# Bias table in bfloat16 column parts, one rwkv gate for four pairs, and a regrouped inversion copy in a two-block network

## The chip, the cores and the metric

The kernel runs on one core of one Trainium2 chip. The metric is the device time of one execution in microseconds (us), lower is better; of several executions the median counts. The engines are TensorE (PE in the profile, with PEld for its weight loads), VectorE (DVE), ScalarE (ACT), GpSimd (POOL) and SyncE (SP, which here only starts DMA transfers).

## The reference, cut to what matters

The network takes 256 tokens of width 1024 through a first block (swiglu feed-forward, a mixer, a second feed-forward) and then two layers of a second block. Three places of it are touched. The first is the rwkv mixer of the first block, above all its gate `g` and its scan:

```python
p = token_shift(p.astype(jnp.float32), mu)
r, k, v, wd, ad, gd = _split_last(
    p, (RWKV_WIDTH, RWKV_WIDTH, RWKV_WIDTH, DECAY_LORA, AAA_LORA, GATE_LORA))
...
g = jax.nn.sigmoid(gd) @ g2          # gd: 256 tokens x 160, g2: 160 x 1024
...
wkv = wkv7_scan(rh, heads(decay), kh, vh, -kk, kk * ah)
...
return (y + bonus.reshape(B, S, RWKV_WIDTH)) * g
```

The second is the bias of the second block's attention, a table of 32 buckets by 8 heads, looked up by the distance of two positions:

```python
def _t5_bias(table, q_pos, k_pos):
    bucket = _t5_bucket(q_pos[:, :, None] - k_pos[:, None, :])
    return jnp.transpose(table[bucket].astype(jnp.float32), (0, 3, 1, 2))
```

## The kernel before

A float32 product is computed on TensorE as three products of float32r operands: each operand is split into a high part (a cast on ACT, L241) and the rest (a subtraction on DVE, L242), and `mm3` (L293 to L295) issues high by high, low by high and high by low. Weights stream through `wload`: SP loads a piece of up to 128x1024 into the ring `wraw` of four buffers, and the split writes the rings `whi` and `wlo`, four buffers each. In the first feed-forward a second ring of raw buffers lets SP run further ahead. The PSUM tiles come from rings too: `acc` (3), `pin` (3), `po` (1) and `pt` (1).

Every engine executes its own instructions strictly in their order. That order isn't the order of the source: a scheduling pass decides it when the program is built, so a change of one place moves instructions around it. Outside of the first feed-forward and the mixer the two programs have the same order.

**Bias table.** While the first feed-forward runs, `bias_steps` (L1138) builds a bias table `bt` in DRAM, in six blocks, about one in each of the feed-forward's eleven column steps. A block is 2048 columns: POOL subtracts the positions (`d`, L1163), DVE compares with the thresholds (`ind`, L1166: 1 where the distance reaches a bucket), and TensorE multiplies `ind` by differences of the table, so that the sum over the reached buckets is the bucket's value. The table's differences are split in two float32r terms, so a block takes four groups of two matmuls (L1170, L1171) of 512 columns. All write the 32 partitions 0 to 31 of a `pt` tile, and after each group ACT copies them (L1172). Four DMAs issued by POOL (L1175) then store the block.

**Mixer.** `mix1` runs eight rwkv pairs (two heads each) in up to three lanes at once, beside a side lane with the dilated attention and the gates, from which TensorE gets dense matmuls to do. `rwkv_setup` computes the inputs of the small matrices once: `lora` matmuls for two halves of the tokens (t), ACT copies the result to `lt` (L727), PE transposes it (L735 to L737), and shift, tanh and a scale make `wdad`, `sga` (128 rows of gd) and `sgb` (32 rows). The gate is computed in each pair: `rwkv_norm` multiplies `sga` and `sgb` by the pair's 128 columns of g2 in plain float32 (L781, L782; a float32 matmul shows as two records), for both halves t, into an `acc` tile that is held until the last multiplication of the pair (L789). The weights g2a and g2b come on ACT's DMA queue.

**Inversion.** Each pair inverts triangular 64x64 matrices in levels (L903 to L937). A level above the first computes eight small products (L908) and two transposes of G (L913) into two `acc` tiles, ACT copies both to `PT`, and the next products (L931) need all of `PT`. The products of o=0 (upper rows) and the transposes share the tile q[0], six blocks wide (copied at L917); those of o=1 have q[1], two blocks wide (copied at L918).

Of the kernel before, what the change touches and what calls it, by code (L numbers as in the profile page):

```python
# [108 lines left out]
def layout(i):  # L109
# [25 lines left out]
    pc[:32, P_MUL + 2] = mu[3328:3360]  # L135
# [9 lines left out]
    o['m_g2'] = i['rwkv_g2'][0]  # L145
# [46 lines left out]
class Net:  # L192
# [518 lines left out]
    def rwkv_setup(self, xT):  # L711
# [13 lines left out]
        lt = rp.tile([128, 2, 512], F32, name="lt", tag="AL", bufs=2)[:, :, :288]  # L725
        for t in range(2):
            nc.scalar.copy(lt[:, t], pins[t])  # L727
        self.wdad = rp.tile([128, T], F32, name="wdad")
        self.sga = rp.tile([128, T], F32, name="sga")
        self.sgb = rp.tile([32, T], F32, name="sgb")  # L730
        p = self.acc([2, T])
        p2 = self.acc([T])
        for t in range(2):
            s = slice(t * 128, t * 128 + 128)
            nc.tensor.transpose(p[:, 0, s], lt[:, t, 0:128], self.idn)  # L735
            nc.tensor.transpose(p[:, 1, s], lt[:, t, 128:256], self.idn)
            nc.tensor.transpose(p2[0:32, s], lt[:, t, 256:288], self.idn)  # L737
        self.shift(self.wdad, p[:, 0], pc[:, P_MUL:P_MUL + 1], om[:, 24:25])
        self.shift(self.sga, p[:, 1], pc[:, P_MUL + 1:P_MUL + 2], om[:, 25:26])
        self.shift(self.sgb, p2[0:32], pc[0:32, P_MUL + 2:P_MUL + 3], om[0:32, 26:27])  # L740
        nc.scalar.activation(self.wdad[0:64], self.wdad[0:64], AF.Tanh)
        for sg in (self.sga, self.sgb):
            nc.scalar.activation(sg, sg, AF.Tanh, scale=0.5)
            nc.vector.tensor_scalar(sg, sg, 0.5, 0.5, op0=ALU.mult, op1=ALU.add)

# [7 lines left out]
    def rwkv_gate(self, hf):  # L753
        nc, rp = self.nc, self.rp
        cs = slice(hf * 512, hf * 512 + 512)
        g2a = rp.tile([128, 512], F32, name="g2a")
        g2b = rp.tile([32, 512], F32, name="g2b")
        nc.scalar.dma_start(g2a, self.I['m_g2'][0:128, cs])
        nc.scalar.dma_start(g2b, self.I['m_g2'][128:160, cs])
        return g2a, g2b, self.gb('m_lnw', 512, 512 * hf), self.gb('m_lnb', 512, 512 * hf)  # L760

    def rwkv_norm(self, yt, vt, bs, pl, g2a, g2b, lnw, lnb):
# [6 lines left out]
        sq = rp.tile([128, 2, 128], F32, name="gsq")  # L769
# [19 lines left out]
        nc.vector.tensor_mul(yt, yt, g)  # L789

    def rwkv_pair(self, p, pl, xT, yt, w2a2, gate):
# [106 lines left out]
        for lv in range(1, 6):  # L898
# [4 lines left out]
            q = [self.acc([4, 64])] if lv == 1 else [self.acc([6, 64]), self.acc([2, 64])]  # L903
# [945 lines left out]
```

## Time and profile before

| what | value |
|---|---|
| median of three executions | 2522.95 us (2520.93 to 2526.31) |
| profiled execution | 2529.44 us |
| its span (first to last instruction) | 2527.7 us |
| mean granted TensorE clock | 0.988 of 2.4 GHz |
| PE busy | 2445.9 us (97%) |
| DVE, ACT, POOL busy | 1123.1, 894.9, 127.1 us |

Busy time counts each instruction from its start to its end. TensorE overlaps matmuls, so two neighbours' starts tell more of what a matmul costs than its own duration. The granted clock is told for stretches: 1.0 is 2.4 GHz, 0.5 is 1.2 GHz. Times in the rows are counted from the first instruction.

### The profile page before, as it was taken

Reading aid. Unit: us, or ns where it says so; the run is one execution under the profiler, and the core shown is the slowest. Engines: PE = TensorE matmul, PEld = TensorE weight load, DVE = VectorE, ACT = ScalarE, POOL = GpSimd, SP = SyncE. Lnnn points to the kernel's source line nnn. Section 1 sums busy time; section 2 is a strip of 40 time slices with the busy share of each in tenths; the row PEclk is TensorE's granted clock in tenths of the full one; section 3 lists DMA queues with packets and bytes.
Section 4 is the critical chain, followed back from the end, with each engine's and each line's share of the span. In section 5 each row is a group of like instructions: output and inputs, shape, how many; then the busy total and the mean of one; then the engine's idle time right before and its main releaser. Section 6 shows DMA issues by size and latency. Waiting matters only on the chain. (4 is left out here: it accounts for less than half of the span.)

```text
span 2527.7 us, 49959 instructions
## 1 busy us (share of the span) xinstructions
PE 2445.9 (97%) x20537; PEld 1739.7 (69%) x20537; DVE 1123.1 (44%) x1991; ACT 894.9 (35%) x1652; POOL 127.1 (5%) x167
## 2 busy tenths in 40 slices
PE   8999999999999999999999999899999999999997
PEld 6778888877788898788888977654356346535631
DVE  7655777665655566875557486401110110000002
ACT  5445544444444466644445564200100010000000
POOL 3200101000000000000001000200000000000000
PEclk9999999999999999999999999999999999999998
DMA  7554222126555454466545435799999999999997
GB/s 271 181 182 154 79 74 84 44 88 233 168 194 191 128 193 134 149 233 200 188 131 185 147 120 178 274 380 394 409 407 399 361 408 393 380 383 408 407 395 293
DMA packets 174379, 607.79 MB, mean 240 GB/s; under 512 B 20288, under 2 KB 25152, under 8 KB 173760
## 3 DMA queue, kind: packets, MB, share of 16 engines
q1 hardware_dynamic: 163872, 584.06, 63.6%
q10 hardware_dynamic: 9232, 18.69, 2.3%
q8 instruction: 163, 2.67, 0.4%
q0 software_dynamic: 1040, 1.78, 0.3%
q14 instruction: 72, 0.59, 0.1%
HBM read 600.78 MB, written 3.67 MB: 239 GB/s over the span
## 5 line engine op out<-in xcount | busy, mean ns | idle before, releaser
L242 DVE TENSOR_TENSOR wlo<-wraw,whi 128x1024 fp32r<-128x1024 f32 (+3 forms) x462 | 554.7, 1205 | 371.0 <-ACT whi L241 360.7
L241 ACT CAST whi<-wraw 128x1024 fp32r<-128x1024 f32 (+3 forms) x462 | 464.5, 1008 | 457.4 <-PE pin L295 225.8
L564 PE MATMUL pin<-wraw,xg 128*32 128x256 f32 (+1 forms) x6272 | 557.0, 411 | 2.3 <-DMA wraw<-e_in 2.3
L564 PEld LDWEIGHTS pin<-wraw,xg 128*32 128x32 f32 (+1 forms) x6272 | 253.0, 113 | 241.1 <-issue 113.5
L293 PE MATMUL pin<-whi,xh 128*128 128x512 f32 (+3 forms) x1088 | 410.3, 377 | 3.2 <-ACT plt L1461 1.4
L294 PE MATMUL pin<-wlo,xh 128*128 128x512 f32 (+3 forms) x1088 | 407.8, 375 | 5.0 <-DVE wlo L242 5.0
L295 PE MATMUL pin<-whi,xl 128*128 128x512 f32 (+3 forms) x1088 | 406.8, 374 | 2.2 <-DVE xl L242 2.1
L549 PE MATMUL acc<-wraw,hT 128*32 128x256 f32 (+1 forms) x3136 | 282.6, 411 | 3.2 <-ACT hT L539 1.7
L572 DVE TENSOR_TENSOR h<-pin,sg 128x256 f32<-128x256 f32 (+1 forms) x84 | 29.9, 378 | 573.8 <-ACT sg L571 573.8
L293 PEld LDWEIGHTS pin<-whi,xh 128*128 128x128 f32 x1088 | 206.4, 190 | 42.1 <-issue 5.6
L295 PEld LDWEIGHTS pin<-whi,xl 128*128 128x128 f32 x1088 | 206.1, 189 | 41.7 <-issue 6.5
L294 PEld LDWEIGHTS pin<-wlo,xh 128*128 128x128 f32 x1088 | 206.4, 190 | 40.0 <-DVE wlo L242 8.7
L549 PEld LDWEIGHTS acc<-wraw,hT 128*32 128x32 f32 (+1 forms) x3136 | 124.8, 113 | 109.3 <-issue 39.8
L571 ACT ACTIVATE sg<-pin 128x256 f32<-128x256 f32 (+1 forms) x84 | 29.4, 350 | 430.7 <-PE pin L564 429.0
L293 PE MATMUL pin<-xh,whi 128*128 128x256 f32 x448 | 131.9, 294 | 0.0
L294 PE MATMUL pin<-xl,whi 128*128 128x256 f32 x448 | 130.2, 291 | 0.0
L295 PE MATMUL pin<-xh,wlo 128*128 128x256 f32 x448 | 128.8, 287 | 0.0
L539 ACT COPY hT<-pt 128x384 f32<-128x384 f32 (+1 forms) x56 | 23.9, 427 | 236.7 <-PE pt L537 236.7
L294 PEld LDWEIGHTS pin<-xl,whi 128*128 128x128 f32 x448 | 86.3, 193 | 1.6 <-issue 0.3
L295 PEld LDWEIGHTS pin<-xh,wlo 128*128 128x128 f32 x448 | 86.4, 193 | 0.7
L293 PEld LDWEIGHTS pin<-xh,whi 128*128 128x128 f32 x448 | 86.3, 193 | 0.7
L295 PE MATMUL acc<-whi,hl 128*128 128x512 f32 x198 | 77.5, 392 | 1.0 <-DVE hl L242 0.9
(524 smaller groups left out, 3097.9 us busy)
## 6 DMA issues: line engine op xcount, KB each, us to landing
wraw<-e_in SPq DMA_DIRECT2D x448, 512.0 KB, 8.7
wraw<-e_out SPq DMA_DIRECT2D x224, 512.0 KB, 8.7
wraw<-ffn_in SPq DMA_DIRECT2D x88, 512.0 KB, 4.1
wraw<-ffn_out SPq DMA_DIRECT2D x44, 512.0 KB, 3.6
wraw<-d_in SPq DMA_DIRECT2D x44, 512.0 KB, 4.3
wraw<-l_dqk SPq DMA_DIRECT2D x32, 512.0 KB, 3.9
wraw<-l_gate SPq DMA_DIRECT2D x32, 512.0 KB, 3.7
wraw<-m_rkv SPq DMA_DIRECT2D x24, 512.0 KB, 3.7
```

Source lines behind the costliest of these rows:

```text
L241: nc.scalar.copy(hi, src)
L242: nc.vector.tensor_sub(lo, src, hi.bitcast(F32))
L293: mm(out, lh, rh, start=start, stop=False, skip_group_check=True)
L294: mm(out, lh, rl, start=False, stop=False, skip_group_check=True)
L295: mm(out, ll, rh, start=False, stop=stop, skip_group_check=True)
L539: nc.scalar.copy(hT[d], pt)
L549: mm(acc[r // per][P[c], r % per], t[:, r * nt + i, P[u]], w[:, n * c:n * c + n], start=d + g + k == 0 and r % per == 0, stop=d == NG // 2 ...
L564: mm(pin[r // per][P[c], r % per].rearrange("p (a c) -> p a c", a=2), xg[:, kc, W * r:W * r + W], v[c * 2 // C][:, c % (C // 2)], start=kc ...
L571: nc.scalar.activation(sg, q[:, :, 0:nh], AF.Silu)
L572: nc.vector.tensor_mul(hs[d][:, b[0]:b[-1] + 1], q[:, :, nh:n], sg)
```

## The change

The bias table's differences become three bfloat16 terms, `ind` becomes bfloat16, and each of a block's four column groups writes 32 partitions of its own: twelve matmuls of 512 columns, term by term over the four column parts, into one `pt` tile, one copy of 128x512, and sixteen stores instead of four. The gate is computed once for four pairs (for 512 columns of g2) with float32r splits, in `rwkv_gate`: its weights come through `wload`, five matmuls of 512 columns for each half t write a `pin` tile, and ACT copies it to SBUF. The rows of `sgb` are duplicated to 64, so that one matmul takes the high and low part. In the inversion the transposes go into the same tile as the products of o=1, whose copy now comes second.

```diff
@@ layout
-    pc[:32, P_MUL + 2] = mu[3328:3360]
+    pc[:64, P_MUL + 2] = np.tile(mu[3328:3360], 2)
...
-    o['m_g2'] = i['rwkv_g2'][0]
+    g2 = np.zeros((2, 128, 1024), np.float32)
+    for hf in range(2):
+        w = i['rwkv_g2'][0][:, 512 * hf:512 * hf + 512]
+        g2[hf, :, :512] = w[:128]
+        g2[hf, :64, 512:] = np.tile(w[128:160], (2, 1))
+    o['m_g2'] = g2
@@ rwkv_setup
-            nc.scalar.copy(lt[:, t], pins[t])
+            nc.scalar.copy(lt[:, t, 0:288], pins[t])
+            nc.scalar.copy(lt[:, t, 288:320], pins[t][:, 256:288])
...
-            nc.tensor.transpose(p2[0:32, s], lt[:, t, 256:288], self.idn)
+            nc.tensor.transpose(p2[0:64, s], lt[:, t, 256:320], self.idn)
...
+        self.sga = [rp.tile([128, T], F32R, name="sga" + e) for e in "hl"]
+        self.split(*self.sga, sga)
+        self.sgb = rp.tile([64, T], F32R, name="sgb")
+        nc.scalar.copy(self.sgb, sgb)
+        nc.vector.tensor_sub(self.sgb[32:64], sgb[32:64], self.sgb[32:64].bitcast(F32))
@@ rwkv_gate
-        g2a = rp.tile([128, 512], F32, name="g2a")
-        g2b = rp.tile([32, 512], F32, name="g2b")
-        nc.scalar.dma_start(g2a, self.I['m_g2'][0:128, cs])
-        nc.scalar.dma_start(g2b, self.I['m_g2'][128:160, cs])
-        return g2a, g2b, self.gb('m_lnw', 512, 512 * hf), self.gb('m_lnb', 512, 512 * hf)
+        (wh, wl), = self.wload(self.I['m_g2'][hf], 1024, [1024])
+        gate = rp.tile([128, 2, 512], F32, name="gate")
+        f = dict(start=False, skip_group_check=True)
+        for t in range(2):
+            s = slice(t * 128, t * 128 + 128)
+            g = self.pin([512])
+            self.mm3(g, self.sga[0][:, s], self.sga[1][:, s], wh[:, 0:512], wl[:, 0:512], True, False)
+            nc.tensor.matmul(g, self.sgb[:, s], wh[0:64, 512:1024], stop=False, **f)
+            nc.tensor.matmul(g, self.sgb[0:32, s], wl[0:32, 512:1024], stop=True, **f)
+            nc.scalar.copy(gate[:, t], g)
+        return gate, self.gb('m_lnw', 512, 512 * hf), self.gb('m_lnb', 512, 512 * hf)
@@ rwkv_norm
-        g = self.acc([2, 128])
-        cs = slice(128 * pl, 128 * pl + 128)
-        for t in range(2):
-            s = slice(t * 128, t * 128 + 128)
-            nc.tensor.matmul(g[:, t], self.sga[:, s], g2a[:, cs], start=True, stop=False)
-            nc.tensor.matmul(g[:, t], self.sgb[:, s], g2b[:, cs], start=False, stop=True)
...
-        nc.vector.tensor_mul(yt, yt, g)
+        nc.vector.tensor_mul(yt, yt, gate[:, :, 128 * pl:128 * pl + 128])
@@ rwkv_pair, a level of the inversion
-            q = [self.acc([4, 64])] if lv == 1 else [self.acc([6, 64]), self.acc([2, 64])]
+            q = [self.acc([4, 64])] if lv == 1 else [self.acc([2, 64]), self.acc([6, 64])]
...
-                    nc.tensor.transpose(q[0][:, 2 + 2 * j:4 + 2 * j].rearrange("p a b -> p (a b)"),
+                    nc.tensor.transpose(q[1][:, 2 + 2 * j:4 + 2 * j].rearrange("p a b -> p (a b)"),
...
-                    nc.scalar.copy(PT[R, 0:6, 0:n], q[0][R, :, 0:n])
-                    nc.scalar.copy(PT[R, 6:8, 0:n], q[1][R, :, 0:n])
+                    nc.scalar.copy(PT[R, 6:8, 0:n], q[0][R, :, 0:n])
+                    nc.scalar.copy(PT[R, 0:6, 0:n], q[1][R, :, 0:n])
@@ bias_steps
-            tbh, tbl = pp.tile([128, 32], F32R, name="tbh"), pp.tile([128, 32], F32R, name="tbl")
+            tb3 = pp.tile([128, 3, 32], BF16, name="tb3")
...
-                    ind = pp.tile([128, 2048], F32R, name="ind")
-                    out = pp.tile([32, 2048], F32, name="bo")
+                    ind = pp.tile([128, 2048], BF16, name="ind")
+                    out = pp.tile([128, 512], F32, name="bo", bufs=2)
...
+                    q = self.pt([512])
+                    for m in range(3):
+                        for n in range(4):
+                            nc.tensor.matmul(q[32 * n:32 * n + 32], tb3[:, m], ind[:, n * 512:n * 512 + 512],
+                                             start=m == 0, stop=m == 2, skip_group_check=True)
+                    nc.scalar.copy(out, q)
+                    m = ni // 4
                     for n in range(4):
-                        s = slice(n * 512, n * 512 + 512)
-                        q = self.pt([512])
-                        nc.tensor.matmul(q[0:32], tbh, ind[:, s], start=True, stop=False)
-                        nc.tensor.matmul(q[0:32], tbl, ind[:, s], start=False, stop=True)
-                        nc.scalar.copy(out[:, s], q[0:32])
-                    for g in range(4):
-                        r = 128 * t + 32 * g + i0
-                        nc.gpsimd.dma_start(self.bt[:, r:r + ni, :nk], out[8 * g:8 * g + 8].rearrange("p (i k) -> p i k", k=nk))
+                        for g in range(4):
+                            nc.gpsimd.dma_start(bt[t, g, :, i0 + n * m:i0 + n * m + m, :nk],
+                                                out[32 * n + 8 * g:32 * n + 8 * g + 8].rearrange("p (i k) -> p i k", k=nk))
```

The scheduler's order moves at the mixer's start. On PE before, the transposes of the first half of `lt` were followed by the first matmuls of pair 0's r projection (`pin<-xh,whi`, weights m_rkv), then came the transposes of the second half:

```order
L295 MATMUL pin<-whi,xl 128x288
L735 MATMUL acc<-c,lt 128x128
L736 MATMUL acc<-c,lt 128x128
L737 MATMUL acc<-c,lt 32x128
L293 MATMUL pin<-xh,whi 128x256
L294 MATMUL pin<-xl,whi 128x256
L295 MATMUL pin<-xh,wlo 128x256
...
L735 MATMUL acc<-c,lt 128x128
```

Now, at the same place on PE, with the lines of the changed kernel (L298 to L300 are `mm3`, L741 to L743 the transposes, L826 and L827 the decay matmuls of pair 0, L775 and L776 the gate's matmuls with `sgb`):

```order
L743 MATMUL acc<-c,lt 64x128
L826 MATMUL acc<-wdad,w2a_2082 128x256
L827 MATMUL acc<-wdad,w2a_2082 128x256
L298 MATMUL pin<-whi,sgah 128x512
L299 MATMUL pin<-wlo,sgah 128x512
L300 MATMUL pin<-whi,sgal 128x512
L298 MATMUL pin<-whi,sgah 128x512
L775 MATMUL pin<-whi,sgb 128x512
L776 MATMUL pin<-wlo,sgb 128x512
...
L298 MATMUL pin<-xh,whi 128x256
```

Both halves' transposes, the decay matmuls and all ten gate matmuls of the first four pairs now stand ahead of pair 0's projections; the decay matmuls stood behind them before.

ACT feeds these matmuls. Before, from the copy of the second half of `lt` on, it had this order (`sga` and `sgb` are done with their tanh, L743):

```order
L727 COPY lt<-pin 128x288
L241 CAST whi<-wraw 128x768
L597 ACTIVATE wdad<-acc,om 128x256
L597 ACTIVATE sgb<-acc,om 32x256
L597 ACTIVATE sga<-acc,om 128x256
L741 ACTIVATE wdad<-wdad 64x256
L743 ACTIVATE sgb<-sgb 32x256
L597 ACTIVATE rT<-pin,om 128x256
L241 CAST whi<-wraw 128x768
L743 ACTIVATE sga<-sga 128x256
```

Now ACT has, from the casts of the gate's weights and of the first two m_rkv pieces (x3) on:

```order
L246 CAST whi<-wraw 128x1024 x3
L732 COPY lt<-pin 128x288
L733 COPY lt<-pin 128x32
L246 CAST whi<-wraw 128x1024
L602 ACTIVATE wdad<-acc,om 128x256
L602 ACTIVATE sg_2055<-acc,om 64x256
L602 ACTIVATE sg_2055<-acc,om 128x256
L747 ACTIVATE wdad<-wdad 64x256
...
L829 ACTIVATE tw<-acc,hw 128x256
L755 CAST sgb<-sg_2055 64x256
L246 CAST sgah<-sg_2055 128x256
```

Pair 0's tanh (`tw`, L829) and the two casts that the gate needs have come in behind the chain; two more tanhs stand where the dots are.

In the inversion, ACT's copies of one level stood in either order before, here with the wide one first:

```order
L917 COPY PT<-acc 128x384
L918 COPY PT<-acc 128x128
L241 CAST whi<-wraw 128x1024
L597 ACTIVATE kT<-pin,om 128x256
L945 COPY XYr<-acc 128x2x64
```

The same place now:

```order
L929 COPY PT<-acc 128x128
L930 COPY PT<-acc 128x384
L829 ACTIVATE tw<-acc,hw 128x256
L832 ACTIVATE sq<-kT,pc 128x256
L830 ACTIVATE ta<-acc,hw 128x256
```

Of the 24 levels of full height (three in each pair) 14 had the narrow copy last; now none has.

## Rows read from the trace of the kernel before

**Rows 1.** The page's busy times, shares of the span and instruction counts.

```profile
PE 2445.9 (97%) x20537; PEld 1739.7 (69%) x20537; DVE 1123.1 (44%) x1991; ACT 894.9 (35%) x1652; POOL 127.1 (5%) x167
```

**Rows 2.** Stretch, its us; busy PE, PEld, DVE, ACT, POOL; granted clock, DMA share, GB/s.

```profile
11.00:216.00 205.00, 200.61 (x887) 158.10 (x887) 129.42 (x134) 104.47 (x143) 40.39 (x39) 0.99 0.56 184
216.00:560.00 344.00, 333.52 (x4140) 281.94 (x4139) 235.19 (x597) 171.32 (x417) 39.33 (x54) 0.97 0.29 91
```

**Rows 3.** Timeline of PE in a bias block: start us, duration us, engine, line, what.

```profile
45.39 0.40 PE L1170 MATMUL pt<-ind,tbh 128*32 128x512 f32 x1
45.62 0.39 PE L1171 MATMUL pt<-ind,tbl 128*32 128x512 f32 x1
45.85 0.39 PE L293 MATMUL pin<-whi,xh 128*128 128x512 f32 x1
```

**Rows 4.** Weight loads of line L1170: count, duration ns min/median/max, first and last start.

```profile
L1170 PEld LDWEIGHTS pt<-ind,tbh x24: 106/106/108, 45.2 to 151.9; 128*32 128x32 f32 x24
```

**Rows 5.** Timeline of PE in the experts, where four column parts take turns.

```profile
1699.50 3.21 PE L564 MATMUL pin<-wraw,xg 128*32 128x256 f32 x56
```

**Rows 6.** Timeline of POOL in the bias blocks, idle time before in brackets.

```profile
51.59 2.46 POOL L1175 DMA_DIRECT2D bt<-bo  x4 [14.95 <-ACT bo L1172]
54.07 3.62 POOL L1163 TENSOR_TENSOR d<-pq,pr 128x2048 int32<-128x2048 int32 x1
71.66 2.40 POOL L1175 DMA_DIRECT2D bt<-bo  x4 [13.98 <-ACT bo L1172]
```

**Rows 7.** Timeline of DVE at the same place.

```profile
51.95 1.22 DVE L242 TENSOR_TENSOR wlo<-wraw,whi 128x1024 fp32r<-128x1024 f32 x1
54.06 4.72 DVE L242 TENSOR_TENSOR wlo<-wraw,whi 128x1024 fp32r<-128x1024 f32 x1 [0.89 <-ACT whi L241]
```

**Rows 8.** Timeline of PE, the gate of the first pair and what follows it.

```profile
314.14 0.38 PE L781 MATMUL acc<-g2a,sga 128*128 128x128 f32 x2
...
315.70 0.46 PE L908 MATMUL acc<-G,AL 64*64 64x64 f32 x16
```

**Rows 9.** Timeline of PE, the gate of the fifth pair.

```profile
459.14 0.74 PE L781 MATMUL acc<-g2a,sga 128*128 128x128 f32 x2
```

**Rows 10.** Busy time and granted clock (PEclk) of three short stretches, columns as in rows 2.

```profile
216.00:220.00 4.00, 2.54 (x14) 1.66 (x13) 4.00 (x7) 2.92 (x7) 0.00 (x0) 0.99 0.68 216
220.00:223.00 3.00, 3.00 (x11) 2.90 (x11) 2.12 (x7) 0.42 (x1) 0.74 (x2) 0.50 0.99 345
...
459.00:469.00 10.00, 10.00 (x64) 8.30 (x64) 6.16 (x20) 2.13 (x5) 2.79 (x4) 0.50 0.01 2
```

**Rows 11.** Timeline of PE at the mixer's start.

```profile
237.01 0.37 PE L293 MATMUL pin<-xh,whi 128*128 128x256 f32 x1
...
238.15 0.28 PE L295 MATMUL pin<-xh,wlo 128*128 128x256 f32 x1
239.46 0.33 PE L735 MATMUL acc<-c,lt 128*128 128x128 f32 x1 [1.04 <-ACT lt L727]
...
239.77 0.36 PE L293 MATMUL pin<-xh,whi 128*128 128x256 f32 x1
```

**Rows 12.** Timeline of ACT at the mixer's start.

```profile
238.06 1.05 ACT L241 CAST whi<-wraw 128x1024 fp32r<-128x1024 f32 x1 [1.08 <-DMA wraw<-m_rkv]
239.02 0.39 ACT L727 COPY lt<-pin 128x288 f32<-128x288 f32 x1
...
240.04 0.48 ACT L597 ACTIVATE wdad<-acc,om 128x256 f32<-128x256 f32 x1
...
243.15 0.41 ACT L743 ACTIVATE sga<-sga 128x256 f32<-128x256 f32 x1
```

**Rows 13.** Timeline of ACT, the two copies of one level of the inversion.

```profile
303.68 0.50 ACT L917 COPY PT<-acc 128x384 f32<-128x384 f32 x1
304.15 0.27 ACT L918 COPY PT<-acc 128x128 f32<-128x128 f32 x1
```

**Rows 14.** Waits of the weight loads from 220 to 560: total us, times, longest.

```profile
PEld acc L931 <- ACT PT L917: 1.5, 6, 0.3
```

More of the change, by code (lines that the diff above doesn't have):

```diff
@@ L724, in rwkv_setup @@
         self.gemm(pins, xT, 8, [I['m_lora'][0, c] for c in range(2)], 288, 4, tiles=True)
-        lt = rp.tile([128, 2, 512], F32, name="lt", tag="AL", bufs=2)[:, :, :288]
+        lt = rp.tile([128, 2, 512], F32, name="lt", tag="AL", bufs=2)[:, :, :320]
         for t in range(2):
-            nc.scalar.copy(lt[:, t], pins[t])
+            nc.scalar.copy(lt[:, t, 0:288], pins[t])
+            nc.scalar.copy(lt[:, t, 288:320], pins[t][:, 256:288])
         self.wdad = rp.tile([128, T], F32, name="wdad")
-        self.sga = rp.tile([128, T], F32, name="sga")
-        self.sgb = rp.tile([32, T], F32, name="sgb")
+        sg2 = rp.tile([128, 2, T], F32, name="sg2", tag="AL", bufs=2)
+        sga, sgb = sg2[:, 0], sg2[0:64, 1]
         p = self.acc([2, T])
@@ L736, in rwkv_setup @@
             nc.tensor.transpose(p[:, 1, s], lt[:, t, 128:256], self.idn)
-            nc.tensor.transpose(p2[0:32, s], lt[:, t, 256:288], self.idn)
+            nc.tensor.transpose(p2[0:64, s], lt[:, t, 256:320], self.idn)
         self.shift(self.wdad, p[:, 0], pc[:, P_MUL:P_MUL + 1], om[:, 24:25])
-        self.shift(self.sga, p[:, 1], pc[:, P_MUL + 1:P_MUL + 2], om[:, 25:26])
-        self.shift(self.sgb, p2[0:32], pc[0:32, P_MUL + 2:P_MUL + 3], om[0:32, 26:27])
+        self.shift(sga, p[:, 1], pc[:, P_MUL + 1:P_MUL + 2], om[:, 25:26])
+        self.shift(sgb, p2[0:64], pc[0:64, P_MUL + 2:P_MUL + 3], om[0:64, 26:27])
         nc.scalar.activation(self.wdad[0:64], self.wdad[0:64], AF.Tanh)
-        for sg in (self.sga, self.sgb):
+        for sg in (sga, sgb):
             nc.scalar.activation(sg, sg, AF.Tanh, scale=0.5)
             nc.vector.tensor_scalar(sg, sg, 0.5, 0.5, op0=ALU.mult, op1=ALU.add)
+        self.sga = [rp.tile([128, T], F32R, name="sga" + e) for e in "hl"]
[3 more added lines that the diff above has]
+        nc.vector.tensor_sub(self.sgb[32:64], sgb[32:64], self.sgb[32:64].bitcast(F32))
     def rwkv_open(self, hf):
@@ L755, in rwkv_gate, with rwkv_norm @@
         cs = slice(hf * 512, hf * 512 + 512)
-        g2a = rp.tile([128, 512], F32, name="g2a")
-        g2b = rp.tile([32, 512], F32, name="g2b")
-        nc.scalar.dma_start(g2a, self.I['m_g2'][0:128, cs])
-        nc.scalar.dma_start(g2b, self.I['m_g2'][128:160, cs])
-        return g2a, g2b, self.gb('m_lnw', 512, 512 * hf), self.gb('m_lnb', 512, 512 * hf)
-    def rwkv_norm(self, yt, vt, bs, pl, g2a, g2b, lnw, lnb):
+        (wh, wl), = self.wload(self.I['m_g2'][hf], 1024, [1024])
[9 more added lines that the diff above has]
+        return gate, self.gb('m_lnw', 512, 512 * hf), self.gb('m_lnb', 512, 512 * hf)
+    def rwkv_norm(self, yt, vt, bs, pl, gate, lnw, lnb):
         nc, rp = self.nc, self.rp
@@ L768, in rwkv_norm @@
         mean, var = rp.tile([128, 2, 2], F32, name="gmean"), rp.tile([128, 2, 2], F32, name="gvar")
-        sq = rp.tile([128, 2, 128], F32, name="gsq")
+        sq = rp.tile([128, 2, 128], F32, name="gsq", tag="sq", bufs=1)
         nc.vector.tensor_reduce(mean, v4(yt), AX, ALU.add)
@@ L930, in rwkv_pair @@
                         for o in range(2):
-                            mm(d[r][B(o), j], PT[B(r), 2 + 2 * j + o, 0:n], PT[B(r), 6 * o + j, 0:n], start=True, stop=True)
+                            mm(d[r][B(o), j], PT[B(r), 2 + 2 * j + o, 0:n], PT[B(r), 6 - 6 * o + j, 0:n], start=True, stop=True)
                 for r in range(2):
@@ L1154, in bias_steps @@
             nc.vector.tensor_sub(tb[:, 0], tb[:, 0], tb[:, 1])
-            self.split(tbh, tbl, tb[:, 0])
+            for n in range(3):
+                nc.vector.tensor_copy(tb3[:, n], tb[:, 0])
+                if n < 2:
+                    nc.vector.tensor_sub(tb[:, 0], tb[:, 0], tb3[:, n])
+            bt = self.bt.rearrange("h (t g i) k -> t g h i k", t=2, g=4)
             for t in range(2):
```

## The prediction

> **What bounds the kernel now.** I read the page's busy times first. TensorE is busy for 97% of the span, DVE for 44%, ACT for 35% [rows 1]. The windows by stretch then say whether that holds where the change works. In the first feed-forward PE is busy for 200.6 of 205 us, with DVE at 129 and ACT at 104; among the rwkv pairs it is 333.5 of 344, with DVE at 235 and ACT at 171 [rows 2]. So both stages wait for PE, and the question for each edit is how much PE time it frees or how long it makes PE stand. Busy counts a matmul until its modelled end, so I price matmuls by the distance of two starts on the timeline, not by their durations.
>
> **The bias table.** A matmul of 512 columns lasts 0.39 us, but the next starts 0.23 us after it [rows 3]. There are 24 of each of the two lines, as the weight loads of one show [rows 4], so before the six blocks cost 48 x 0.23 = 11.0 us of PE. Now they have 72 matmuls. All write 32 partitions, four neighbours four different column parts. The nearest thing in the trace is the expert stage, which has float32 matmuls in four column parts: 56 records of 256 float32 columns lie in 3.21 us [rows 5]. Less about 0.4 for the last one's own duration that leaves 2.8 us for 13 steps of four records, 0.218 us a step. One float32r matmul of 512 columns takes 0.23, so a step of four costs what a single matmul of 512 columns does: the four column parts run side by side there. By that row 72 matmuls are 18 groups of 0.218, 3.9 us; the edit frees 7.1 us. That they don't run side by side is a rival below. I take the experts' row since it has the same column parts and a step of the same length.
>
> What else a block does lies under PE's work. ACT has one copy of 512 columns in place of four. DVE's comparison writes bfloat16 in place of float32r; its cost isn't shown, from nothing to twice a like instruction, and DVE is idle for 76 of 205 us [rows 2]. POOL issues sixteen DMAs in place of four: 2.46 us become 4 x 2.46 = 9.8, and the subtraction behind them, 3.62 us, starts later [rows 6]. Together they are 13.4 us, and blocks come every 20.1 us (51.59 to 71.66), so POOL keeps pace and the store of the table, needed only by the second block, can't be late. One thing could hurt: while POOL subtracts, a DVE subtraction takes 4.72 us in place of 1.22 [rows 7], 3.5 us longer. The pause is there before as well, only at another place relative to PE. I count nothing for moving it; a rival has its price.
>
> **The gate.** Before, a pair's eight records take 314.14 to 315.70, 1.56 us at full clock [rows 8]. Seven pairs make 10.9 us. The fifth runs in a stretch granted 0.50, that is 1.2 GHz, and its first two records take 0.74 in place of 0.38 [rows 9, 10]; I count it double, 3.1, so 14.0 us in all. Now there are twenty matmuls of 512 columns, 20 x 0.23 = 4.6 us. PE is freed of 9.4 us. The weights' splits (two casts, two subtractions) and four copies are ACT and DVE work of about 1 us each, under PE's, as [rows 2] show these engines' idle time; without that cover the second gate would cost PE one cast and two copies, some 2 us.
>
> **The wait at the mixer's start.** This speaks against the change. The order shows that ten gate matmuls and the decay matmuls now stand ahead of pair 0's projections on PE, and whatever is behind them waits as well. Before, PE began these projections at 237.01, worked until 238.15, waited until 239.46 for the copy of the second half of `lt`, and went on at 239.77 [rows 11]. That copy itself was late by a weight cast whose DMA had not landed: the cast starts at 238.06, the copy at 239.02 [rows 12]. Now, in the times of before: the copy starts at 239.02; with the small one behind it (0.2, an estimate from half the big one's 0.39) ACT is free at 239.6. The order puts one more weight cast there, 1.05, so the chain starts at 240.65. Before, the first and the eighth ACT instruction of this place started at 240.04 and 243.15 [rows 12]; one of the seven steps is a weight cast of 768 columns (0.8, an estimate from 1.05 for 1024), which leaves 2.3 for six, 0.39 each. Nine of them (three shifts, three tanhs, `tw`, two casts) take 3.5, to 244.2, and the subtractions of the low parts on DVE take two such steps more, to 245.0. Then seven of the ten gate matmuls are left, 1.6, and the projections start at 246.6: 9.6 us later than before. Of this, 2.3 is the gate (counted above), about 1.0 are ten transpose and decay records that before stood elsewhere (three transposes take 0.31, 239.46 to 239.77), and 1.2 is the old wait, gone. PE stands 5.1 us longer. Bounds: 4.0, if the missing DMA lands earlier (ACT waited 1.08 for it [rows 12], and ACT's queue no longer loads gate tables); 6.1, if one more cast of 1.05 gets in.
>
> **The clock.** After 216 to 220, in which PE was busy for only 2.54 of 4 us, the granted clock fell to 0.50 [rows 10]. The new wait leaves PE emptier than that. The fall costs nothing while PE waits and half of what it does afterwards; for the 3 us after that wait which the rows show at 0.50, 1.5 us. Bounds: nothing, and half of a stretch of 10 us like that at 459, 5.0 [rows 10].
>
> **The inversion.** The narrow copy behind the wide one made `PT` ready at 304.42 in place of 304.18 [rows 13]. In 14 of 24 levels it stood so; that is 0.24 x 14 = 3.4 us over the chains of all pairs, in up to three lanes under PE's other work. What PE's weight loads waited for the wide copy is 1.5 us [rows 14]. Bounds: nothing and 1.5; I take 0.8, the middle, for nothing tells which of the six waits had the narrow copy in the way. Which lane gets an `acc` tile when also changes, and I have no row for a price of that.
>
> **Sum**, against the profiled execution's 2529.44: -7.1 - 9.4 + 5.1 + 1.5 - 0.8 = -10.7, to 2518.7. The median of before is 6.5 below that execution; the same difference from 2522.95 gives **2512.2 us**, 0.4% less. About 0.2% (5 us) is what a measurement of this kernel can tell from no change.
>
> **Rivals.** *One after another* (slower). If each weight load of a bias matmul waits until the matmul before it has ended, nothing overlaps: 12 x (0.39 + 0.11) = 6.0 us a block by [rows 3, 4], 36.0 in place of 11.0. The sum becomes 7.1 + 25.0 - 10.7 = +21.4, 2544.4. The other four terms make -3.6, so the kernel gets slower from 1.83 + 3.6 / 6 = 2.4 us a block on, and by more than 0.2% from 3.3. Against it: [rows 5], where loads belong to column parts too. If only the array is shared in turn, at 0.23 each, the blocks cost 72 x 0.23 = 16.6 and the sum is 5.6 - 3.6 = +2.0, 2525.0. The Trainium skill, page "TensorE: Matmul & The Clock Gate", Part 3 on packing small matmuls, has a rule for this rival: a weight load overlaps matmuls in flight only when its row group differs, and here all of them use the same rows; by that rule the time would be this rival's 2544, and [rows 5], where neighbours use the same rows too, do not bear it out. The same part also tells of 2.38 times the speed with three column parts, by which the twelve matmuls would overlap.
>
> *DVE's pause* gets in PE's way: of the six subtractions the four that stand behind a block's stores move, and each keeps a weight's low part back for the 3.5 us of [rows 7], +14.0, 2526.3. For it: PE has few pieces in stock. Against it: the same pause came before and PE's share of that stage is 98% [rows 2].
>
> *A deeper start*: wait 6.1, clock 5.0, the second gate uncovered 2.0, no gain in the inversion: -3.4 in sum, 2519.6.
>
> *A lighter start*: wait 4.0, no fall of the clock, inversion 1.5: -14.0, 2509.0; and if the slow stretch of 459 to 469 leaves together with the old gate's records in it, 5.0 less, 2504.
>
> *It does not do what it says*: the copies' order is free already. That is 0.8 of my sum and changes no verdict.
>
> **Chances.** My forecast 0.58, the lighter start 0.10, the deeper one 0.16, DVE's pause 0.06, turns in the array 0.04, one after another 0.06. The range from 2504 to 2522 takes in the two starts and leaves out the last three rivals, 0.16, and little below. Within 0.2% (2517.9 to 2528.0) end the deeper start, the pause, the turns and 0.03 of my forecast: 0.29. Faster: 0.65. Slower: 0.06.
>
> **What would show it.** In the changed profile, a block's twelve matmuls start within about 0.7 us (2.8 or 6 for the first rival); the lines L781 and L782 are gone and ten matmuls with `sgah`, `sgal` and `sgb` of about 0.23 us each stand in two places; PE has a hole of some 6 us around 230 to 240, before pair 0's projections, and the clock is 0.50 after it; POOL's DMAs take about 10 us a block; the stages after the mixer last as before. I am wrong if PE's hole is filled by other work or grows to twice that, or if the rwkv pairs with their new order wait more on each other than these rows let me see.

## The result, and the profile after

The changed kernel takes **2552.03 us** (median of 5 runs, 2547.50 to 2554.34); the kernel before, on the same chip, 2524.67 (2520.93 to 2526.31). The ratio is 1.0106 (95% interval 1.0094 to 1.0117): some 27 us slower, where 11 us faster was forecast. In the text, shares of a ratio are turned into time with 2524 us. The profiled execution of the changed kernel took 2552.97 us, its span is 2551.0.

First the page's busy times and the two stretches of [rows 1, 2], in the changed kernel:

```profile
PE 2453.5 (96%) x20517; PEld 1745.1 (68%) x20517; DVE 1127.6 (44%) x1999; ACT 888.9 (35%) x1643; POOL 163.5 (6%) x239
```

```profile
11.00:216.00 205.00, 199.70 (x944) 158.88 (x943) 136.08 (x154) 98.97 (x132) 77.24 (x113) 1.00 0.60 195
216.00:560.00 344.00, 323.80 (x3960) 271.57 (x3959) 221.45 (x553) 166.13 (x400) 37.55 (x50) 0.93 0.27 82
```

The first stretch is as full as before. In the second, PE is busy 10 us less and at a lower granted clock, 0.93 in place of 0.97. Most of the loss is there.

The bias table answers to [rows 3, 4]. PE's timeline in one block, and the rows of its line in the whole program (count, duration ns min/median/max, first and last start):

```profile
44.91 0.83 PE L1187 MATMUL pt<-ind,tb 128*32 128x512 bf16 x12
45.67 0.51 PE L298 MATMUL pin<-whi,xh 128*128 128x512 f32 x1
```

```profile
L1187 PEld LDWEIGHTS <-tb x72: 92/95/97, 44.9 to 134.5; 128*32 128x32 bf16 x72
L1187 PE MATMUL pt<-ind,tb x72: 379/379/389, 44.9 to 134.8; 128*32 128x512 bf16 x72
```

Twelve matmuls that last 0.38 each hold PE for 0.76 us (44.91 to 45.67): the column parts run side by side, and six blocks cost 4.6 us in place of 11.0.

The mixer's start answers to [rows 11]. PE's timeline: the first half's transposes, the second half's, the decay matmuls, the first gate matmul, pair 0's first projection. Under it two stretches of windows (columns as in [rows 2]):

```profile
228.50 0.27 PE L741 MATMUL acc<-c,lt 128*128 128x128 f32 x1
...
231.28 0.33 PE L741 MATMUL acc<-c,lt 128*128 128x128 f32 x1 [2.29 <-ACT lt L732]
...
234.78 0.79 PE L826 MATMUL acc<-wdad,w2a 64*128 64x256 f32 x1 [2.95 <-ACT wdad L747]
...
237.16 0.80 PE L298 MATMUL pin<-whi,sgah 128*128 128x512 f32 x1 [1.15 <-ACT sgah L246]
...
243.20 0.58 PE L298 MATMUL pin<-xh,whi 128*128 128x256 f32 x1
```

```profile
228.00:244.00 16.00, 9.61 (x29) 5.03 (x28) 8.88 (x14) 10.32 (x21) 0.00 (x0) 0.63 0.40 131
244.00:250.00 6.00, 6.00 (x32) 6.00 (x32) 1.58 (x2) 2.36 (x4) 0.44 (x1) 0.56 0.28 87
```

PE works through this line in order and waits three times in it. The mean granted clock is 0.63 while it waits, and still 0.56 in the 6 us after, when the projections could run.

The second gate, PE first, then what reads the old gate (DVE) and what stores the new one (ACT):

```profile
359.34 0.39 PE L298 MATMUL pin<-whi,sgah 128*128 128x512 f32 x1
...
375.73 0.50 PE L298 MATMUL pin<-whi,sgah 128*128 128x512 f32 x1
...
377.06 0.50 PE L776 MATMUL pin<-wlo,sgb 32*128 32x512 f32 x1
377.48 0.38 PE L298 MATMUL pin<-xh,whi 128*128 128x256 f32 x1
```

```profile
445.02 0.42 DVE L801 TENSOR_TENSOR ya<-ya,gate 128x256 f32<-128x256 f32 x1
```

```profile
445.48 1.07 ACT L777 COPY gate<-pin 128x512 f32<-128x512 f32 x2
```

The two sums are finished at about 361 and 377.5, and they are copied out at 445.48, right after pair 3's norm has read the first gate. Why is theory W of the experiments.

Last, the end of the program. The DRAIN rows of POOL's queue (durations min/median/max; the longest is the one that follows POOL's last work), of the kernel before and of the changed one:

```profile
L1845 POOLq DRAIN  x3: 40/113/3367, 2522.1 to 2527.4; - x3
```

```profile
L1864 POOLq DRAIN  x3: 40/113/9249, 2540.9 to 2550.7; - x3
```

Before, the long one starts at 2522.1 and is over some 2.2 us ahead of the end; now it starts at 2540.9 and is over 0.9 us ahead of it, later than what the other engines do, and the end waits for it.

### The profile page after: what moved, and what is told of

It is laid out like the page before. It is cut to its first block, busy times and chain, and to the rows that moved or that the text cites. A ratio compares the mean times of both kernels' runs of the same rounds, so it can differ in the third digit from the quotient of the medians.

```text
span 2551.0 us, 50005 instructions
## 1 busy us (share of the span) xinstructions
PE 2453.5 (96%) x20517; PEld 1745.1 (68%) x20517; DVE 1127.6 (44%) x1999; ACT 888.9 (35%) x1643; POOL 163.5 (6%) x239
## 3 DMA queue, kind: packets, MB, share of 16 engines
q0 software_dynamic: 3216, 1.78, 0.3%
## 5 line engine op out<-in xcount | busy, mean ns | idle before, releaser
L298 PE MATMUL pin<-whi,xh 128*128 128x512 f32 (+3 forms) x1088 | 412.3, 379 | 3.8 <-ACT plt L1480 1.4
L300 PE MATMUL pin<-whi,xl 128*128 128x512 f32 (+3 forms) x1088 | 407.5, 375 | 3.1 <-DVE xl L247 3.0
L298 PEld LDWEIGHTS pin<-whi,xh 128*128 128x128 f32 x1088 | 207.4, 191 | 43.2 <-issue 8.4
L300 PEld LDWEIGHTS pin<-whi,xl 128*128 128x128 f32 x1088 | 207.1, 190 | 42.3 <-issue 6.5
L298 PE MATMUL pin<-xh,whi 128*128 128x256 f32 x448 | 133.9, 299 | 0.8 <-DVE vT L603 0.6
L300 PE MATMUL pin<-xh,wlo 128*128 128x256 f32 x448 | 129.9, 290 | 0.0
L298 PEld LDWEIGHTS pin<-xh,whi 128*128 128x128 f32 x448 | 87.9, 196 | 4.3 <-issue 2.2
L300 PEld LDWEIGHTS pin<-xh,wlo 128*128 128x128 f32 x448 | 87.7, 196 | 0.3
```

What stands on the lines that cost most here:

```text
L298: mm(out, lh, rh, start=start, stop=False, skip_group_check=True)
L300: mm(out, ll, rh, start=False, stop=stop, skip_group_check=True)
```

## The experiments

Each was timed against the kernel before on its own chip. The ratio has its 95% interval behind it, 0.09% to 0.19% to either side; the difference of two ratios has a wider one, 3 to 5 us.

**1. The bias table alone** (old gate, old inversion; its diff is the part `bias_steps` of the change).

> The kernel before with the new bias table alone (old gate, old inversion). Theory A (the loss is the gate's: PE stands at the mixer's start and then works at half clock): the first feed-forward ends 8 us earlier and nothing gives it back, 2516 us (2514 to 2519), mixer from lora transposes to the first yb transposes 339 us as before. Rival D (whoever arrives 8 us earlier at the mixer meets late weights or another clock, whatever the gate): the mixer is longer than 345 us and the whole 2523 or more.

Measured: 2522.97 us, ratio 0.9996 (0.9987 to 1.0005). Theory A's time did not come, and rival D's came without its reason. The first feed-forward ends 8 us earlier (the first transposes of `lt` at 229.03 in place of 236.8) and the mixer is not longer, 335 us. But from PE's last matmul to the end it takes 18.0 us in place of 13.4: POOL's DRAIN of 9.25 us. So the matmuls' gain was there and 4.6 us went back at the end.

**2. The gate alone** (diff: `rwkv_setup`, `rwkv_gate`, `rwkv_norm` of the change).

> The kernel before with the new gate alone (old bias table, old inversion). Theory A: the whole loss and the 8 us that the bias edit gained are the gate's, so 2559 us (2555 to 2563). Rival C (the inversion's new order of copies and its acc tiles cost most of the second loss between 366 and 480 us): 2546 us (2540 to 2552).

Measured: 2555.49 us, 1.0128 (1.0109 to 1.0146), inside theory A's range. The loss is the gate's, 32 us.

**3. The first gate later.**

```diff
-                            w2a2, gate = self.rwkv_open(started // 4), self.rwkv_gate(started // 4)
+                            w2a2, gate = self.rwkv_open(started // 4), []
+                            if started:
+                                gate += self.rwkv_gate(started // 4)
@@ rwkv_pair, after the three projections
+        if p == 0:
+            gate += self.rwkv_gate(0)
```

> The changed kernel with the first gate emitted after pair 0's three projections in place of before them. Theory A: PE has projections to do while the gate's chain runs, the 13.5 us lost at the mixer's start come back: 2538 us (2534 to 2542), and if the later loss of 13 us is only the clock's echo of that start, 2525 us. Rival B (the shared sq buffer ties the lanes together) and rival C (inversion) also leave the later 13 us, but say that the start alone gives back no more than 5 us: 2547 us.

Measured: 2534.95 us, 1.0037 (1.0022 to 1.0053): 17 us back, more than the 13.5 expected, and inside theory A's range. PE's timeline and windows at the place of the hole:

```profile
229.55 0.37 PE L298 MATMUL pin<-xh,whi 128*128 128x256 f32 x1
```

```profile
228.00:244.00 16.00, 15.69 (x117) 15.06 (x115) 12.14 (x18) 12.01 (x23) 0.00 (x0) 1.00 0.73 242
```

The projections start 13.7 us earlier, PE is full, the clock is whole. The later loss stays: from the matmul that broadcasts pair 3's norms (`rnb`, 343.15) to that of pair 6's (466.91) it takes 123.8 us, in the kernel with the bias alone 109.8.

**4. The norm's squares in memory of their own.**

```diff
-        sq = rp.tile([128, 2, 128], F32, name="gsq", tag="sq", bufs=1)
+        sq = self.ga[:, :, 128 * pl:128 * pl + 128]
```

> The changed kernel with the norm's squares in memory of their own (a slice of the second gate's tile, unused until 626 us) in place of the sq buffer of the pairs. Theory A: the buffer is not what anybody waits for, 2552 us as the changed kernel (2549 to 2555). Rival B (the shared buffer delays the pairs between 366 and 480 us): the later 13 us come back, 2540 us (2536 to 2545).

Measured: 2554.14 us, 1.0117 (1.0099 to 1.0136). Rival B falls.

**5. Twenty-four stores in place of 96**, bias alone:

```diff
-        self.bt = self.dr.tile([8, T, T], F32, name="bt")
+        self.bt = self.dr.tile([2, 32, 32, T], F32, name="bt")
...
-                        for g in range(4):
-                            nc.gpsimd.dma_start(bt[t, g, :, i0 + n * m:i0 + n * m + m, :nk],
...
+                        nc.gpsimd.dma_start(self.bt[t, :, i0 + n * m:i0 + n * m + m, :nk],
...
@@ bias_load: eight loads in place of two
+                nc.scalar.dma_start(self.btab[32 * g:32 * g + 32, :, 128 * t:128 + 256 * t],
+                                    self.bt[t, 8 * g:8 * g + 8, :, :128 + 128 * t].rearrange("h i k -> i h k"))
```

> The new bias table alone, with its scratch in memory laid out so that one store takes the 32 rows of a column part: 24 stores on POOL's queue in place of 96, and eight loads of the table in place of two. Theory E (the new bias frees about 6 us of PE, but POOL's last DRAIN grows with the stores that POOL has issued, 3.37 us after 28 and 9.25 us after 100, and then ends the program 4.6 us later): the DRAIN is back at about 3.4 us and the time is 2518.4 us (2516 to 2520.5), against 2523.0 with the bias alone. Rival (the DRAIN is longer for another reason, or the table frees nothing): 2523 us as the bias alone.

Measured: 2523.29 us, 0.9987 (0.9975 to 0.9999). The DRAIN is 3.367 us as expected, and the last matmul lies 13.6 us ahead of the end. The time hardly moved, and it is the rival's, though not for the rival's reason. Most of what the DRAIN gives back is lost where the table is loaded: DVE's `x<-acc,x` ahead of the loads starts 2.6 us later than in number 1 (849.91 against 847.34), its `ru<-lat,rope` behind them 6.3 us later (901.91 against 895.62), so 3.7 us are lost between. ACT's timeline there, first number 5, then number 1:

```profile
866.91 1.32 ACTq L1193 DMA_DIRECT2D btab<-bt  x3
868.27 0.91 ACT L241 CAST whi<-wraw 128x864 fp32r<-128x864 f32 x1 [0.89 <-issue]
```

```profile
861.23 0.91 ACT L241 CAST whi<-wraw 128x864 fp32r<-128x864 f32 x1
```

The cast of the next weights stands 7.0 us later, behind the issues of the eight loads and in another order of ACT's work. Which of the two costs more was not tried apart.

**6. No new gate** (new bias table and new inversion).

> The changed kernel with the gate of before (new bias table and new inversion stay). If the inversion's new order costs nothing, 2523 us as the bias alone (2521 to 2525). Rival C (its copies or its acc tiles cause the loss of some 12 us between 345 and 480 us): 2530 us or more.

Measured: 2522.04 us, 0.9983 (0.9974 to 0.9991), as expected. The inversion costs nothing; against number 1 it gains 0.13%, 3 us, which is no more than the interval of that difference.

**7. Late gate, old inversion.**

> The kernel with the late first gate, and the inversion of before. If the 12 us that it still loses between 345 and 480 us belong to the gate: 2535 us as the late gate (2532 to 2537). Rival C (the inversion beside the gate causes them): 2525 us or less.

Measured: 2538.32 us, 1.0048 (1.0034 to 1.0062). It lies 1 us above the range; rival C falls. Again the new inversion is some 3 us the better one, here inside the interval of the difference, 5 us.

**8. No second gate.** Late first gate; pairs 4 to 7 use the first one.

```diff
-                                gate += self.rwkv_gate(started // 4)
+                                gate += [gate0[0], self.gb('m_lnw', 512, 512), self.gb('m_lnb', 512, 512)]
...
```

> The kernel with the late first gate, without the second gate: pairs 4 to 7 are multiplied by the gate of pairs 0 to 3, so that half of the gate's result is wrong; its weights, casts and ten matmuls are left out. If the second gate in its place, at pair 4's start, causes the loss between 345 and 480 us: 2525 us (2522 to 2528). If the loss comes from elsewhere (the new order of all pairs, the lanes' waits and the clock that falls after them), only the second gate's ten matmuls go: 2532 us (2530 to 2535).

Measured: 2516.11 us, 0.9959 (0.9942 to 0.9975), below both ranges. That is 0.78%, 20 us, below number 3, though ten matmuls are worth only some 3. So far I read it as a matter of place, since pair 4's projections start at 365.06 with the second gate and at 344.52 without it.

**9 to 12. The other ring, and another place.** Number 9 is number 3 with this; 11 is the changed kernel with this alone; 12 is number 9 with the stores of number 5:

```diff
-            g = self.pin([512])
+            g = self.acc([512])
```

Number 10 is the changed kernel with both gates after the projections (`if pl == 0: gate += self.rwkv_gate(p // 4)` in `rwkv_pair`).

> The kernel with the late first gate, and both gates' sums in the acc ring in place of the pin ring. Theory P (the second gate's second half must wait for a pin tile until the side lane's product of two tiles is copied out, and pair 4's projections, whose tiles come after it in the ring, wait with it: they start 20 us later than without the second gate): the halves follow each other, pair 4's projections start near 348 us, and the time is 2517 us (2514 to 2521) against 2535 with the pins. Rival Q (the second gate costs by its work and its place, whatever ring; in acc it also stands in the way of the lanes' small products): 2528 us or more.

> The changed kernel with both gates emitted after the projections of pair 0 and of pair 4, in the pin ring as the changed kernel has it. Theory P: pair 4's projections have their pin tiles before the gate's, nothing of pair 4's early chain stands behind the gate, 2518 us (2515 to 2523). Rival Q: the work of the second gate costs as much here, 2530 us or more.

> The changed kernel with nothing but the gates' sums in the acc ring; both gates are called where the change calls them. Theory P: the 20 us of the second gate go, and of the 18 us of the first one as much as the other ring lets pair 0's projections pass: 2533 us (2529 to 2537) if PE still stands at the mixer's start as in the changed kernel, 2518 us if the projections get ahead of the gate. Rival Q: 2545 us or more.

> Late first gate, sums in the acc ring, and the bias table's 24 merged stores. Theories P and E together: 4.5 us less than the kernel with the late gate in the acc ring, by POOL's last DRAIN, 2512.5 us (2509 to 2517). If the merged stores give nothing back, as much as that kernel.

Measured: number 9 2570.47 us, 1.0175 (1.0158 to 1.0191); number 10 2531.63, 1.0024 (1.0012 to 1.0037); number 11 2570.61, 1.0169 (1.0152 to 1.0187); number 12 2571.43, 1.0175 (1.0159 to 1.0190). Theory P failed in all four; 9 to 11 lie on rival Q's side, and 12 is as number 9, so that the merged stores gave nothing back there. In number 10 pair 4's projections start at 345.14, as they do without a second gate, and the second gate's ten matmuls stand together (369.50 to 372.56), yet most of the loss is still there: 15 of 18 us, against number 14 below. In `acc` it is 35 us worse than in `pin`. (In number 11 pair 0's projections start at 229.19, ahead of the gate's matmuls, so that it lacks the wait at the mixer's start and equals number 9.) The row that explains both is that of the copies out of the sums, in numbers 3, 10 and 9 (its last start stands behind "to"):

```profile
L779 ACT COPY gate<-pin x4: 567/585/592, 245.0 to 433.6; 128x512 f32<-128x512 f32 x4
```

```profile
L777 ACT COPY gate<-pin x4: 567/585/592, 245.5 to 428.7; 128x512 f32<-128x512 f32 x4
```

```profile
L779 ACT COPY gate<-acc x4: 580/586/591, 245.8 to 473.9; 128x512 f32<-128x512 f32 x4
```

The copies belong to matmuls that end the sums between 348 and 373 us. `gate` is made with `rp.tile([128, 2, 512], F32, name="gate")` in a pool of one buffer. The second gate goes into the memory of the first, which pair 3's norm reads last; until then the two sums keep two of the ring's three tiles. Out of `pin` the projections and the side lane are fed, out of `acc` every small product of the lanes. That is theory W.

**13 to 15. A place of its own for the second gate's result**, in the changed kernel (13), with the late first gate (14), with the late first gate and the `acc` ring (15). `self.ga` is the tile of a gate that is computed later, behind the pairs; each half of it takes one result:

```diff
-        gate = rp.tile([128, 2, 512], F32, name="gate")
+        gate = self.ga[:, :, cs]
```

> The changed kernel with the second gate's result in memory of its own (a half each of a later gate's tile, unused until 626 us) in place of one tile for both. Theory W (the copies of the second gate's sums wait for the last reader of the first gate, and the sums keep two of three pin tiles for 86 us): the copies follow the products at once, the loss after 345 us goes, and only the loss at the mixer's start stays, 2534 us (2530 to 2539). Rival Q (the second gate costs by its work and place): 2550 us as the changed kernel.

> Late first gate and the second gate's result in memory of its own. Theory W: 2518 us (2515 to 2521), the kernel without a second gate and its ten matmuls of 2.3 us. Rival Q: 2533 us as the late gate.

> As the late gate with its sums in the acc ring (2570 us), with the second gate's result in memory of its own. Theory W: what made the acc ring worse are two of three acc tiles held for 109 us; they come free at once, and the time is 2519 us (2515 to 2525). Rival Q (the gate's products in the acc ring stand in the lanes' way): 2560 us or more.

Measured: number 13 2532.74 us, 1.0029 (1.0017 to 1.0041); number 14 2518.42, 0.9966 (0.9954 to 0.9979); number 15 2522.59, 0.9985 (0.9975 to 0.9995). All three lie inside theory W's ranges, and number 15 is 48 us below number 9, number 14 18 us below number 3 and number 13 19 us below the changed kernel, each by this one line. The copies of number 14:

```profile
L779 ACT COPY ga<-pin x4: 568/582/588, 247.5 to 352.8; 128x512 f32<-128x512 f32 x4
```

The stretch in which number 9 held its two `acc` tiles, first number 9, then number 15:

```profile
364.00:474.00 110.00, 89.47 (x868) 70.40 (x864) 49.37 (x115) 37.45 (x83) 10.44 (x14) 0.79 0.21 65
```

```profile
364.00:474.00 110.00, 106.33 (x1411) 89.64 (x1410) 75.95 (x199) 54.55 (x138) 13.46 (x19) 0.97 0.25 75
```

With the tiles held PE has 868 recorded matmuls in 110 us, with the tiles free 1411, at a granted clock of 0.97 in place of 0.79. So held tiles cost twice: PE stands idle for 20.5 us of the 110 in place of 3.7, and what it then does is granted less clock. No row names a wait for a free PSUM tile. That the buffer is the cause is shown by the three pairs of runs; that the way from it to the loss is the held tiles, and not another effect of the scheduler's new order, is argued from the late copies and from the two rings' different losses.

**16 to 18. The stores again.** Number 16 is number 14 with the stores of number 5 and the eight loads on POOL's queue. Numbers 17 (on number 14) and 18 (on number 6) keep two loads and merge the stores by two dense tables:

```diff
+        self.bt = [self.dr.tile([8, 128, 128 + 128 * t], F32, name=f"bt{t}") for t in range(2)]
...
+                        nc.gpsimd.dma_start(self.bt[t].rearrange("h (g i) k -> g h (i k)", g=4)[:, :, (i0 + n * m) * nk:(i0 + n * m + m) * nk],
+                                            out[32 * n:32 * n + 32])
```

> Late first gate, the second gate's result in memory of its own, 24 merged stores of the bias table, and its eight loads on POOL's queue, not ACT's. Theories W and E: the last DRAIN of POOL is 4 us in place of 9.25 and no longer the end, and the 6.5 us that eight loads on ACT's queue cost near 865 us do not come: 2513.5 us (2510 to 2517). If the loads on POOL's queue are late too: 2518 us or more.

> Late first gate, the second gate's result in memory of its own, 24 merged stores of the bias table into two dense tables, and two loads of it on ACT's queue as in the changed kernel. Theory E: POOL's last DRAIN is 3.4 us, nothing is given back near 865 us, and the time is 4.4 us below the kernel with 96 stores: ratio to before 0.9949 (0.993 to 0.996), 2513 us. Rival (what ends the program is within a us of POOL's DRAIN anyway, or the fewer, larger stores cost elsewhere): 0.9966 as with 96 stores.

> New bias table with these 24 merged stores and two loads, new inversion, gate of before. Theory E: 4.4 us below the same kernel with 96 stores (ratio 0.9983): 0.9965 (0.995 to 0.998), and so 4 us above the kernel with the mended gate, which frees PE of the old gate's products. Rival: 0.998 as with 96 stores.

Measured: number 16 2516.93 us, 0.9964 (0.9952 to 0.9977); number 17 **2515.00**, 0.9956 (0.9942 to 0.9969); number 18 2520.26, 0.9973 (0.9962 to 0.9985). All three lie inside their ranges, number 16 at the edge and with the ratio of number 14. The DRAINs of 16 and 17:

```profile
L1868 POOLq DRAIN  x3: 46/113/4017, 2508.9 to 2514.4; - x3
```

```profile
L1866 POOLq DRAIN  x3: 40/113/3367, 2513.2 to 2518.7; - x3
```

In number 16 the loads land late: the table is first added to on DVE at 875.8, in number 17 at 864.0. In the trace of number 17 the end comes 4.4 us sooner after the last matmul than in that of number 14 (13.65 in place of 18.05). Of the whole time numbers 17 and 18 each gain 0.10%, 2.5 us, on their kernels with 96 stores; the intervals hold 4.4 and also nothing, so that the sign of this last step is likely but not settled. Number 17 is 0.44% faster than the kernel before, the lowest ratio of all; those of 14 and 16 lie inside its interval.

## Why the prediction was wrong, step by step

**By parts.** From ratio to ratio, times 2524 us: bias table -1.0 (number 1), inversion -3.3 (6 against 1), a mended gate -4.3 (14 against 6), the first gate in its place +15.9 (13 against 14), the second gate's held tiles +19.4 (the changed kernel against 13). They add up to the measured +26.7 by construction, for each starts from the ratio of the one before it. The bias table's has 2.3 us to either side, the others 3 to 4: the two gate losses are clear of that, the three gains are not, or only just.

**The step that failed most: the gate's splits and copies "are ACT and DVE work of about 1 us each, under PE's".** I counted what the four copies cost ACT and not what they wait for: the overlap failed, not the duration. The new tile `gate` has one buffer, whose last reader comes 85 us after the first of the second gate's sums is done, and the sums stand in a ring of three meanwhile. That is 19.4 us, which the sum had at nothing. The price of an uncovered second gate, 2 us in *a deeper start*, was off by a factor of ten. The diff and the pool's `bufs=1` would have shown it; the closing sentence, that the pairs may "wait more on each other than these rows let me see", named the risk without its place.

**The wait at the mixer's start** was right in its mechanism and nearly in its size. PE stands there three times, for 2.29, 2.95 and 1.15 us, in place of once for 1.04 [rows 11]: 5.4 us more, where 5.1 was forecast. What failed at this place is **the clock**, 1.5 us with 5.0 as its bound. I priced half clock for 3 us after the wait, by [rows 10]; here it fell during the wait and held until 249.1. The ten gate matmuls took 6.0 us (237.16 to 243.20), where the late gate's ten take 3.4 at full clock, and I had let only seven of them stand behind the chain, for 1.6 us. The first projections then start 0.21 us apart (243.58, 243.79) in place of 0.12 (number 3, 230.22, 230.34); 27 of them take 5.9 us in place of some 3.2. So the clock costs 2.7 us in the gate and about as much behind it, some 5.4. The projections start 13.9 us later (243.20) than with the bias alone (229.28), where 9.6 was forecast. The rest comes later: number 3 keeps PE fuller from 250 to 300 us, here below the changed kernel, and these 3.4 us the sum did not have.

```profile
250.00:300.00 50.00, 46.17 (x524) 41.17 (x526) 35.73 (x78) 24.84 (x52) 8.49 (x9) 1.00 0.36 112
```

```profile
250.00:300.00 50.00, 49.55 (x659) 43.14 (x657) 39.28 (x91) 27.00 (x67) 5.76 (x7) 0.97 0.26 81
```

These three make 14.2 us. By numbers 13 and 3 the first gate in its place costs 15.9 to 17.4, in place of 6.6; what the rest is, the rows leave open.

**The bias table.** The column parts run side by side, as [rows 5] had it: 0.76 us a block, 4.6 for all six, where 3.9 was forecast, so 6.4 us freed. *One after another* and *turns* fall. By an estimate from the rule of the Trainium skill that stood beside the first (page "TensorE: Matmul & The Clock Gate", Part 3) a block would take 6.0 us; the trace has 0.76 and does not agree. I counted POOL's sixteen issues by their duration (9.8 us forecast, 8.7 in the trace, and the store was in time) and not the end of the program, where the DRAIN takes back 4.6. *DVE's pause* did not show: in the traces of the kernels with the new table the first feed-forward ends 5.7 to 8.3 us earlier.

**The gate's products.** Forecast 9.4 us freed, 14.0 less 4.6. The ten matmuls of a gate take 3.4 us, so 6.7 for both, because those with `sgb` cost more (below): 7.3 freed at full clock. In the changed kernel they took 9.4, with the clock's 2.7 us of above in it; a mended gate gains 4.3 by the runs.

**The inversion**, -0.8 forecast with 1.5 as its bound, is about -3 in both pairs of runs, with 3 and 5 us to either side. The sign fits; whether it is more than the waits of [rows 14] is not settled, nor was it tried which part of it gains (the copies' order or the ring).

**"The stages after the mixer last as before"** holds for the work on PE within some 3 us (from the first transpose of `yb` to the end of the last matmul 1936.3 us before, 1939.6 after); the DRAIN is what it left out.

## What to carry to other kernels

Where a change keeps a result longer, ask for each new tile how many buffers it has, who reads its old content last, and what is stuck in front of it until then: two PSUM sums that waited for one SBUF buffer cost 19 us in one ring and 48 in the other, and one line undid it. Work that a long chain feeds belongs behind work that is ready, on an engine that runs in order. And a change that issues more small transfers is read to the last row of the program, not only where it issues them.

## What the runs showed of the hardware

POOL's DRAIN at the end grows with the number of transfers that POOL issued, long after they landed: 3.37 us with 28, 4.02 with 36 and 9.25 with 100, that is 0.081 and 0.082 us for each. Neither bytes nor packets do it: that queue moved 1.78 MB before and after, and numbers 5 and 17 and the kernel before, with 28 transfers each, have the same 3.37 us with 912, 2064 and 1040 packets.

The two `sgb` matmuls of a half, with weights of 64 and 32 rows, cost PE nearly twice what their neighbours with 128 rows do. PE's timeline of number 14, and that of its weight loads:

```profile
348.23 0.39 PE L298 MATMUL pin<-whi,sgah 128*128 128x512 f32 x1
348.46 0.39 PE L299 MATMUL pin<-wlo,sgah 128*128 128x512 f32 x1
...
349.01 0.49 PE L777 MATMUL pin<-whi,sgb 64*128 64x512 f32 x1
349.43 0.49 PE L778 MATMUL pin<-wlo,sgb 32*128 32x512 f32 x1
349.85 0.61 PE L298 MATMUL pin<-whi,xh 128*128 128x384 f32 x2
```

```profile
348.23 0.19 PEld L299 LDWEIGHTS pin<-wlo,sgah 128*128 128x128 f32 x1
348.46 0.19 PEld L300 LDWEIGHTS pin<-whi,sgal 128*128 128x128 f32 x1
349.01 0.18 PEld L777 LDWEIGHTS pin<-whi,sgb 64*128 64x128 f32 x1 [0.36 <-issue]
349.43 0.18 PEld L778 LDWEIGHTS pin<-wlo,sgb 32*128 32x128 f32 x1 [0.24 <-issue]
```

The starts are 0.23 us apart with 128 rows, and 0.42 with 64 and with 32. A load of 128 rows behind a matmul of 128 rows starts with that matmul, so it is done when the next can begin. Where the number of rows changes (128 to 64, 64 to 32, 32 to 128), the load starts only with its own matmul, 0.33 to 0.42 us after the start of the one before. Few rows alone don't cost that: among the experts of the same trace float32r matmuls of 256 columns with 32 rows, two at a time on different rows, start 0.12 us apart one after another, as pair 0's projections of 256 columns with 128 rows do in number 3.

```profile
1738.28 0.28 PE L1684 MATMUL pin<-vl,ohT 32*128 32x256 f32 x2
1738.39 0.27 PE L1684 MATMUL pin<-vh,ohT 32*128 32x256 f32 x2
1738.51 0.28 PE L1684 MATMUL pin<-vl,ohT 32*128 32x256 f32 x2
```

So the trace puts the price on the change of the number of rows; no run changes that alone.
